# Another order of query tiles for attention's last two heads

## The chip, the cores and the metric

The kernel runs on one core of a Trainium2 chip. The metric is the device time of one execution in microseconds. Three runs of the kernel before took 2134.39 to 2135.3 us, with a median of 2135.06 us; beside them stands one execution under the profiler.

## The reference, cut to what matters

The program is one inference step of a two-layer decoder trunk over a prompt of 2048 positions and 64 sample positions, with 1024 channels. Layer 0 runs a pooling mixer and a differential attention side by side, layer 1 is a gated linear attention. The change touches the attention of the prompt and the output projection behind it:

```python
def block(args):                                   # 16 blocks of 128 queries
    qi, bi = args
    sc = jnp.einsum('bqhcd,bkhcd->bhcqk', qi, k)    # 4 heads, two score maps (c) each
    sc = jnp.where(causal, sc, -jnp.inf)
    p = jax.nn.softmax(sc, axis=-1)
    a = p[:, :, 0] - lam_full * p[:, :, 1]
    return jnp.einsum('bhqk,bkhe->bqhe', a, v)
...
o = rms_norm(o, subln_w) * (1.0 - lam_init)
mix = jnp.concatenate([pool_out * silu(pg), o * silu(ag)], axis=-1)
y = layer_norm(DN_ALPHA * x + mix @ w_out, ln_g, ln_b)
```

A block of queries needs no other block. Under the causal mask block t looks at t + 1 blocks of keys, so its work grows with t. A row of the output projection needs all four heads of its own position, and layer 1 needs the rows of layer 0.

## The kernel before, in words

Layer 0's input projection comes first, then attention head by head, each with other work woven in: head 0 with the pooling half of the output projection, head 1 with the sample positions, heads 2 and 3 together with the attention half of the output projection. That last stage, some 300 us long, is the one that changes. The first matmuls of layer 1 follow it.

A **tile** t is 128 queries, t from 0 to 15; two tiles with one number halved are a **pair** (pair 7 is tiles 14 and 15). Queries and gates are loaded by pairs, results are scaled by pairs. For one tile and one head `scores` makes two **score maps** (c = 0 and 1). From tile 8 on a map is four pieces of equal width, two to a PSUM tile of 128 x 2 x 512; there are two such PSUM tiles (`sc`, the pool has two buffers). For each piece TensorE multiplies the high and the low part of the queries with the keys (L1016, L1017), VectorE takes the maximum of a PSUM tile (L1021) and, with two of them, the smaller of the two negated maxima (L1034); ScalarE writes exp to SBUF (L1036), which frees the PSUM tile. VectorE then combines the two maps (L1045). Tiles 4 to 7 need one PSUM tile for a map, tiles 0 to 3 one for both.

`pv` follows a tile behind: transposes of 128 x 128 (L1068, `tp`), copies by ScalarE (L1073, `aT`), products with the values (L1061, `po`), and at the end of a pair the scale and the gate on GpSimd (`oq`, L1097 and L1099).

`out_attention` makes the **output tiles**. Number i is the 128 positions of tile i; number 16 is the sample. An output tile is four transposes (L1227, `otp`: two of the heads 0 and 1 that were stored, one each of heads 2 and 3), a split in high and low (L1231, L1232), 24 products of 512 columns (`op`, L51 to L53), sums on VectorE (L1281), a LayerNorm with three passes over 128 x 1024 on GpSimd (L1302 to L1304), a store, and eight transposes (L1245, `oyp`) for layer 1. It waits for `oq` of its pair and for its own loads (`om`, `oz`, three buffers for `oz`).

Two things set the order. `units` and `out_attention` are generators that `weave` draws from in proportion to their costs; an output tile is given out only when head 3 has finished the tile behind its pair (`A.done`). The instructions so recorded are then ordered by a scheduler with its own model of time; scores have a higher priority. Each engine works through its own list in that order. Before, tiles go 0 to 15 and output tiles 0 to 13, then 16, 14, 15.

Of the kernel before, what the change touches and what calls it, by code (L numbers as in the profile page):

```python
# [394 lines left out]
def layers(tc, d):  # L395
# [6 lines left out]
    with ExitStack() as left:  # L402
# [12 lines left out]
        for m, j in project_even(tc, d, P, P2, W, slot, psf):  # L415
# [8 lines left out]
            elif (m, j) == (5, 3):  # L424
                A.room_weights()
                units = A.units([0], [1])
# [15 lines left out]
    with ExitStack() as left:  # L442
        wp = left.enter_context(tc.tile_pool(name="aow", bufs=4, **rw))
        op = left.enter_context(tc.tile_pool(name="ao", bufs=2, **rw))
        sm = left.enter_context(tc.tile_pool(name="aosm", bufs=4, **rw))
        A.mixp = op
        O = Odd(tc, d, odd, keep, A.ident, P2, psf, fill_banks)

        def last():
            yield from A.units([2, 3], [])  # L450
            O.first_weights()
            yield from A.drain()
            A.over = True

        fill = out_attention(tc, d, A, wp, op, sm)
        weave(last(), fill, 2 * HEAD_COST, 17 * (8 * 640 + 1320.0), drain=False)
        right.close()
        O.start()
        for _ in fill:
            pass  # L460
# [423 lines left out]
class Attention:  # L884
# [166 lines left out]
    def pv(self, t, h, a, s1, place):  # L1051
# [51 lines left out]
            rs = slice(128 * (t - 1), 128 * t + 128)  # L1103
            nc.gpsimd.dma_start(self.d["mixa"][rs, 128 * h:128 * h + 128].rearrange("(c p) e -> p c e", p=128), oq)
        if h == 3:
            self.done = t
        yield 100

    def units(self, heads, after):


        for t in range(16):
            for h in heads:
                if t % 4 == 2 and t < 14:
                    self.load_kv(h, t // 4 + 1)
                if t % 2 == 1 and t < 15:
                    self.load_q(h, t // 2 + 1)
                if t == 14 and h == heads[0]:
                    for n in after:
                        self.load_kv(n, 0)  # L1120
                        self.load_q(n, 0)
                old = self.pend.pop(0) if len(self.pend) == 2 else None
                for c in self.scores(t, h):
                    yield c
                    c = next(old, None) if old else None
                    if c is not None:
                        yield c
                if old:
                    yield from old
                self.pend.append(self.pv(t, h, *self.cur))  # L1130
# [4 lines left out]
        self.pend = []  # L1135


HEAD_COST = 76000.0


# [55 lines left out]
def out_attention(tc, d, A, wp, op, sm):  # L1196
# [24 lines left out]
    def tile_(i, mt, m, z):  # L1221
        t0, n = TT[i]
        c = m.shape[1]
        tp = A.fill_tile(f"otp{i}")
        for k in range(4):
            src = m[:, 128 * k:128 * k + 128] if 128 * k < c else A.mix[i // 2, k][:, i % 2, :]
            nc.tensor.transpose(tp[:, 128 * k:128 * k + n], src, ident[:n, :n])  # L1227
        tv = tp.rearrange("p (k t) -> p k t", k=4)[:, :, :n]
        mh = op.tile([128, 4, 128], F32R, tag="oh", name=f"oh{i}")
        ml = op.tile([128, 4, 128], F32R, tag="ol", name=f"ol{i}") if i < 16 else mh[:, :, n:]  # L1230
        nc.scalar.activation(mh[:, :, :n], tv, AF.Copy)  # L1231
        nc.vector.tensor_tensor(out=ml[:, :, :n], in0=tv, in1=mh[:, :, :n], op=ALU.subtract)  # L1232
        yield 440
        ln = LayerNorm(tc, mt.bitcast(BF16)[:n], sm, z, 1.0, g[:n], b[:n], f"o0_{i}")
        yield from out_mm(nc, A.fill_tile, f"op{i}", n, mh, ml, w, ln.add)
        ln.finish(d["y0"][t0:t0 + n, :], i in (14, 15))
        zs[i] = z

    def turn(i):
# [9 lines left out]
            nc.scalar.dma_start(d["y0T"][4 * q:4 * q + 4, :, t0:t0 + n].rearrange("k p t -> p k t"), yt[:, :, :n])  # L1249
            yield 440  # L1250

    order = list(range(14)) + [16, 14, 15]
    ahead = load(order[0])
    for j, i in enumerate(order):
        while A.done < min((i | 1) + 1, 15) if i < 16 else not A.over:
            yield None
        now, ahead = ahead, load(order[j + 1]) if j < 16 else None
        yield from tile_(i, *now)
# [1176 lines left out]
```

## Time and profile before

| what | value |
|---|---|
| median of three runs | 2135.06 us |
| profiled execution, its own time | 2130.93 us |
| its span | 2129.1 us |
| mean granted TensorE clock | 0.981 |
| first and last score matmul of heads 2 and 3, tile 4 on | 907.66 and 1192 us |
| first product of output tile 14 | 1220.74 us |

The profile is read by engine: PE is TensorE's matmuls, PEld its weight loads, DVE is VectorE, ACT ScalarE, POOL GpSimd, SP the queue that issues most loads. A row of a timeline begins with the start and the duration in us; in square brackets stands how long the engine had been idle and what ended it. A row of a group ends with busy us, mean ns and idle us.

### The profile page before, as it was taken

The page shows a single profiled execution, that of the slowest core. Times are in us where ns is not written, and L with a number is a line of the kernel's source. Part 1 is how long each engine was busy: PE and PEld are TensorE (multiplying, and loading weights), DVE is VectorE, ACT ScalarE, POOL GpSimd, SP SyncE. Part 2 cuts the span into 40 slices and gives each one's busy share as a digit, 9 for nine tenths or more (in the row PEclk, how much of TensorE's full clock was granted, in tenths as well). Part 3 has the DMA queues.
Part 4 walks back from the last instruction along what each step waited for, and adds up shares of the span by engine and source line. Part 5 has one row for each costly group of instructions (what it writes and reads, how often), then busy time and mean ns, then how long its engine had stood idle before and what let it go on. Part 6 is the DMA issues. An engine that isn't in the chain of part 4 may idle for free.

```text
span 2129.1 us, 31464 instructions
## 1 busy us (share of the span) xinstructions
PE 1999.4 (94%) x10769; PEld 1633.9 (77%) x10769; DVE 1487.7 (70%) x2762; ACT 1022.1 (48%) x1922; POOL 876.6 (41%) x1163
## 2 busy tenths in 40 slices
PE   8999998999899999888898899999999898999998
PEld 7878786877688777667786688788887676788886
DVE  7697657564876676798767666666734547888884
ACT  4144433345633465664555533435527755555552
POOL 2345445323854542666543513222111122466554
PEclk9999999999999999999999999999999998999998
DMA  8877777447964598563321558665543457555532
GB/s 288 270 250 239 256 261 236 162 110 191 296 203 149 170 299 290 153 197 118 115 70 65 167 183 284 241 221 197 190 154 109 161 167 246 176 173 199 167 127 110
DMA packets 210972, 407.75 MB, mean 192 GB/s; under 512 B 29186, under 2 KB 106370, under 8 KB 210802
## 3 DMA queue, kind: packets, MB, share of 16 engines
q1 hardware_dynamic: 140354, 234.57, 36.2%
q0 software_dynamic: 49664, 156.39, 20.7%
q10 hardware_dynamic: 20784, 14.68, 2.2%
q8 instruction: 87, 1.43, 0.3%
q14 instruction: 83, 0.68, 0.1%
HBM read 277.99 MB, written 127.55 MB: 190 GB/s over the span
## 4 chain that ended last, share of the span: by engine, by line
PE 54%; DVE 15%; DMA 12%; issue 6%; ACT 6%; POOL 4%; SPq 1%; ACTq 0%; POOLq 0%; DVEq 0%
PE f L52 9%; PE f L51 9%; PE f L53 9%; PE po L1061 3%; PE sc L1016 2%; PE sc L1017 2%; ACT e L1036 2%; PE tp L1068 2%; DVE nm L1021 2%; DMA wr<-pt 2%; PE zp L51 1%; PE zp L53 1%; PE zp L52 1%; PE gz L53 1%; PE gz L51 1%
## 5 line engine op out<-in xcount | busy, mean ns | idle before, releaser
L1036 ACT ACTIVATE e<-sc,nm 128x896 f32<-128x896 f32 (+11 forms) x192 | 165.0, 865 | 126.4 <-DVE nm L1034 88.0
L1021 DVE TENSOR_REDUCE nm<-sc 128x1 f32<-128x768 f32 (+7 forms) x160 | 156.6, 990 | 27.1 <-PE sc L1017 16.7
L45 DVE TENSOR_TENSOR wk<-wr,wk 128x1024 fp32r<-128x1024 f32 x80 | 98.1, 1228 | 99.0 <-ACT wk L40 98.8
L45 DVE TENSOR_TENSOR wl<-wr,wh 128x1024 fp32r<-128x1024 f32 (+1 forms) x90 | 108.6, 1210 | 79.3 <-ACT wh L40 70.1
L1016 PE MATMUL sc<-kst,qh 128*128 128x512 f32 (+9 forms) x352 | 133.4, 382 | 29.7 <-ACT e L1036 28.3
L1061 PE MATMUL po<-vt,aT 128*128 128x128 f32 x1088 | 153.1, 280 | 3.6 <-ACT aT L1073 2.2
L40 ACT ACTIVATE wh<-wr 128x1024 fp32r<-128x1024 f32 (+1 forms) x85 | 88.0, 1038 | 137.3 <-PE f L52 67.6
L1061 PEld LDWEIGHTS po<-vt,aT 128*128 128x128 f32 x1088 | 138.1, 194 | 10.5 <-ACT aT L1073 2.5
L40 ACT ACTIVATE wk<-wr 128x1024 fp32r<-128x1024 f32 x77 | 81.2, 1058 | 131.1 <-PE f L53 94.0
L1073 ACT ACTIVATE aT<-tp 128x512 f32<-128x512 f32 (+3 forms) x160 | 85.5, 534 | 97.9 <-PE tp L1068 97.3
L1017 PE MATMUL sc<-kst,ql 128*128 128x512 f32 (+9 forms) x352 | 121.8, 349 | 0.0
L1016 PEld LDWEIGHTS sc<-kst,qh 128*128 128x128 f32 x352 | 67.5, 192 | 50.0 <-ACT e L1036 40.8
L1068 PE MATMUL tp<-ident,e 128*128 128x128 f32 x544 | 91.3, 282 | 12.1 <-ACT aT L1073 10.5
L1045 DVE SCALAR_TENSOR_TENSOR e<-e,c,e 128x128 f32<-128x128 f32 (+15 forms) x64 | 95.6, 1494 | 1.4
L1068 PEld LDWEIGHTS tp<-ident,e 128*128 128x128 f32 x544 | 63.8, 144 | 27.4 <-ACT aT L1073 15.4
L1017 PEld LDWEIGHTS sc<-kst,ql 128*128 128x128 f32 x352 | 67.7, 192 | 4.0 <-issue 0.2
L1039 DVE TENSOR_TENSOR s<-s 128x1 f32<-128x1 f32 x64 | 21.1, 330 | 68.3 <-ACT e L1036 68.0
L1092 POOL TENSOR_SCALAR s1q<-s 128x1 f32<-128x1 f32 x64 | 16.9, 267 | 102.6 <-DVE s L1039 87.6
L53 PE MATMUL op<-wh,ol 128*128 128x512 f32 x128 | 52.1, 407 | 5.0 <-DVE ol L1232 5.0
L51 PE MATMUL op<-wh,oh 128*128 128x512 f32 x128 | 53.0, 414 | 1.2 <-ACT oh L1231 1.1
L51 PE MATMUL zp<-wh,zh 128*128 128x512 f32 x128 | 52.1, 410 | 0.0
L51 PE MATMUL gz<-wh,gmh 128*128 128x512 f32 x128 | 51.6, 407 | 0.0
(882 smaller groups left out, 6669.7 us busy)
## 6 DMA issues: line engine op xcount, KB each, us to landing
wr<-in_w_q SPq DMA_DIRECT2D x75, 512.0 KB, 4.9
wr<-pt SPq DMA_DIRECT2D x40, 512.0 KB, 7.6
wr<-rt SPq DMA_DIRECT2D x40, 512.0 KB, 4.5
sk<-in_cachek SPq DMA_DIRECT2D x64, 256.0 KB, 3.8
sv<-in_cachev SPq DMA_DIRECT2D x64, 256.0 KB, 4.8
pt<-pn POOLq DMA_DIRECT2D x32, 256.0 KB, 7.0
qr<-q SPq DMA_DIRECT2D x64, 128.0 KB, 4.1
kr<-k SPq DMA_DIRECT2D x32, 256.0 KB, 4.5
```

The source lines that it names most:

```text
L40: h = nc.scalar.activation(hi, raw, AF.Copy)
L45: return h, (lo_eng or nc.vector).tensor_tensor(out=lo, in0=raw, in1=hi, op=ALU.subtract)
L51: nc.tensor.matmul(ps, lh(k), rh(k), start=(first and k == 0), stop=False, **kw)
L52: nc.tensor.matmul(ps, lh(k), rl(k), start=False, stop=False, **kw)
L53: nc.tensor.matmul(ps, ll(k), rh(k), start=False, stop=(last and k == n - 1), **kw)
L1016: nc.tensor.matmul(o, qh[:, c, qs], kst[:, ks], start=True, stop=False)
L1017: nc.tensor.matmul(o, ql[:, c, qs], kst[:, ks], start=False, stop=k < npc - 1)
L1021: nc.vector.tensor_reduce(out=nm[:, c, i:i + 1], in_=p[:, :, :w], op=ALU.max, axis=AX.XY, negate=True)
L1036: nc.scalar.activation(o, p, AF.Exp, bias=nm[:, m, 0:1], accum_out=s[:, m, i if npc > 1 else 0:][:, :1])
L1045: nc.vector.scalar_tensor_tensor(out=es[0][:, :nk], in0=es[1][:, :nk], scalar=c2, in1=es[0][:, :nk], op0=ALU.mult, op1=ALU.add)
L1061: nc.tensor.matmul(po, s[:, 128 * j:128 * j + 128], vt[:, k0 + j, :], start=(k0 + j == 0), stop=(k0 + j == n - 1))
L1068: nc.tensor.transpose(p[:, 128 * j:128 * j + 128], a[:, 128 * (k0 + j):128 * (k0 + j) + 128], self.ident)
```

## The change

`units` takes a list of tiles. Heads 2 and 3 get the list `TILES`, the pairs 0, 1, 2, 7, 3, 6, 4, 5 with two tiles each. `out_attention` goes through its output tiles by the same list, 16 ahead of the last two, and `A.done` counts finished tiles instead of naming the last one. Since tile 14 now comes seventh, the blocks of keys and values are asked for at positions 0, 1 and 3 of the list, where they were asked for at tiles 2, 6 and 10. The urgent form of the LayerNorm, which stays off GpSimd, goes with the last two of the list: 10 and 11.

```diff
-            yield from A.units([2, 3], [])
+            yield from A.units([2, 3], [], TILES)
...
         if h == 3:
-            self.done = t
+            self.done += 1
...
-    def units(self, heads, after):
-        for t in range(16):
+    def units(self, heads, after, order=range(16)):
+        order = list(order)
+        mixed = order != sorted(order)
+        for n, t in enumerate(order):
             for h in heads:
-                if t % 4 == 2 and t < 14:
-                    self.load_kv(h, t // 4 + 1)
-                if t % 2 == 1 and t < 15:
-                    self.load_q(h, t // 2 + 1)
+                if mixed:
+                    if n in (0, 1, 3):
+                        self.load_kv(h, 1 + (0, 1, 3).index(n))
+                elif n % 4 == 2 and n < 14:
+                    self.load_kv(h, n // 4 + 1)
+                if n % 2 == 1 and n < 15:
+                    self.load_q(h, order[n + 1] // 2)
...
+TILES = [t for i in (0, 1, 2, 7, 3, 6, 4, 5) for t in (2 * i, 2 * i + 1)]
...
-        ln.finish(d["y0"][t0:t0 + n, :], i in (14, 15))
+        ln.finish(d["y0"][t0:t0 + n, :], i in TILES[14:])
...
-    order = list(range(14)) + [16, 14, 15]
+    order = TILES[:14] + [16] + TILES[14:]
...
-        while A.done < min((i | 1) + 1, 15) if i < 16 else not A.over:
+        while A.done < min(TILES.index(i | 1) + 1, 15) if i < 16 else not A.over:
```

What this makes of the engines' lists is shown at three places. In the names the first number is the tile and the second the head; for scores the third is the map.

TensorE, around tile 14. Before, the second map of head 3 (`sc14_3_1`), up to tile 15:

```order
L1061 MATMUL po13_3_12191<-vt3_8755,aT13_3_12_12256 128x128 x2
L1227 MATMUL otp12_12469<-ident_4353,oq12_2_11841 128x128
L1016 MATMUL sc14_3_1_0_12221<-kst3_1_8747,qh3_7_11851 128x480
...
L1068 MATMUL tp14_2_0_12292<-ident_4353,e14_2_0_12083 128x128
L1016 MATMUL sc14_3_1_1_12238<-kst3_1_8747,qh3_7_11851 128x480
...
L1068 MATMUL tp14_2_0_12292<-ident_4353,e14_2_0_12083 128x128 x3
L1068 MATMUL tp14_2_4_12310<-ident_4353,e14_2_0_12083 128x128 x4
L1061 MATMUL po14_2_12291<-vt2_8735,aT14_2_0_12297 128x128 x4
L1016 MATMUL sc15_2_0_0_12285<-kst2_0_8726,qh2_7_11754 128x512
```

Now, the first map of head 2 (`sc14_2_0`) and what stands up to its second:

```order
L1016 MATMUL sc14_2_0_0_10189<-kst2_0_8726,qh2_7_9974 128x480
...
L1234 MATMUL otp1_9801<-ident_4353,om1_9745 128x128 x2
L1234 MATMUL otp1_9801<-ident_4353,oq0_2_9500 128x128
L1016 MATMUL sc14_2_0_1_10209<-kst2_0_8726,qh2_7_9974 128x480
...
L1061 MATMUL po4_3_10049<-vt3_8755,aT4_3_0_10055 128x128 x4
L51 MATMUL op1_0_9811<-wh101_9279,oh1_9806 128x512
...
L53 MATMUL op1_1_9825<-wh104_9305,ol1_9807 128x512
L1068 MATMUL tp5_2_0_10199<-ident_4353,e5_2_0_9982 128x128 x3
L1016 MATMUL sc14_2_1_0_10251<-kst2_1_8727,qh2_7_9974 128x480
```

Before, tile 14's four maps have no product of an output tile among them. Now all 24 products of output tile 1 stand between two maps of tile 14, and those of output tile 2 between the next two.

TensorE, behind the second map of tile 8 and head 3 (`sc8_3_1`). Before:

```order
L1017 MATMUL sc8_3_1_1_10732<-kst3_1_8747,ql3_4_10390 128x288
L1245 MATMUL oyp2_1_10269<-ident_4353,oz2_9767 128x128 x4
L1227 MATMUL otp4_10451<-ident_4353,om4_10121 128x128 x2
L1061 MATMUL po7_2_10546<-vt2_8735,aT7_2_4_10577 128x128 x4
L1068 MATMUL tp7_3_0_10650<-ident_4353,e7_3_0_10397 128x128 x4
L51 MATMUL op4_0_10461<-wh101_9271,oh4_10456 128x512
```

Now:

```order
L1017 MATMUL sc8_3_1_1_11796<-kst3_1_8747,ql3_4_11410 128x288
L1068 MATMUL tp13_3_4_11768<-ident_4353,e13_3_0_11417 128x128 x4
L1061 MATMUL po13_3_11749<-vt3_8755,aT13_3_0_11755 128x128 x4
L1068 MATMUL tp13_3_8_11785<-ident_4353,e13_3_0_11417 128x128 x4
L1061 MATMUL po13_3_11749<-vt3_8755,aT13_3_4_11773 128x128 x4
L1016 MATMUL sc9_2_0_0_11852<-kst2_0_8726,qh2_4_11312 128x320
```

Here 21 products of output tile 4 stood behind this map; now only transposes and value products of tile 13 do.

SP's list of loads, ahead of the first weight of the output projection (`wr101`). `kr2_3` is the last block of keys of head 2, `vt3` are values of head 3. Before:

```order
L963 DMA kr2_2_10153<-k0_58 64x2x512 x2
L963 DMA kr3_2_10249<-k0_58 64x2x512 x2
L989 DMA sga2_1_9450<-sg0_60 128x2x128
L963 DMA kr2_3_11015<-k0_58 64x2x512 x2
L963 DMA kr3_3_11152<-k0_58 64x2x512 x2
L951 DMA vt3_8755<-v0_59 128x4x128
L2246 DMA mixa_62<-ssq_9231 8x8x128 x4
```

Now:

```order
L989 DMA sga2_1_9474<-sg0_60 128x2x128
L977 DMA qr3_2_9701<-q0_57 64x2x256 x2
L963 DMA kr2_2_9459<-k0_58 64x2x512 x2
L963 DMA kr3_2_9507<-k0_58 64x2x512 x2
L963 DMA kr2_3_9641<-k0_58 64x2x512 x2
L963 DMA kr3_3_9693<-k0_58 64x2x512 x2
L951 DMA vt3_8755<-v0_59 128x4x128 x4
```

The scheduler had put the key loads this early already. Of the four value loads of head 3, two stood behind the output weights; now all four are ahead of them.

More of the change, by code (lines that the diff above doesn't have):

```diff
@@ L1105, in pv @@
         if h == 3:
-            self.done = t
+            self.done += 1
         yield 100
-    def units(self, heads, after):
-        for t in range(16):
+    def units(self, heads, after, order=range(16)):
+        order = list(order)
+        mixed = order != sorted(order)
+        for n, t in enumerate(order):
             for h in heads:
-                if t % 4 == 2 and t < 14:
-                    self.load_kv(h, t // 4 + 1)
-                if t % 2 == 1 and t < 15:
-                    self.load_q(h, t // 2 + 1)
[L1118 to L1121, printed above, removed]
+                if mixed:
[5 more added lines that the diff above has]
+                    self.load_q(h, order[n + 1] // 2)
+                if n == 14 and h == heads[0]:
+                    for x in after:
+                        self.load_kv(x, 0)
+                        self.load_q(x, 0)
                 old = self.pend.pop(0) if len(self.pend) == 2 else None
```

## The prediction

> **What bounds the kernel now.** I read the engine totals first, then the stage of heads 2 and 3 in stretches, then the starts of its score maps.
>
> ```profile
> PE 1999.4 (94%) x10769; PEld 1633.9 (77%) x10769; DVE 1487.7 (70%) x2762; ACT 1022.1 (48%) x1922; POOL 876.6 (41%) x1163
> ```
>
> TensorE is the busiest engine, but its busy time holds pipelined ends; what counts is how far apart matmuls start. The prices, from PE's timeline in the stage:
>
> ```profile
> 1128.09 0.39 PE L51 MATMUL op<-wh,oh 128*128 128x512 f32 x1
> 1128.32 0.39 PE L52 MATMUL op<-wl,oh 128*128 128x512 f32 x1
> ...
> 1133.26 0.60 PE L1068 MATMUL tp<-ident,e 128*128 128x128 f32 x4
> 1133.70 1.06 PE L1061 MATMUL po<-vt,aT 128*128 128x128 f32 x8
> 1134.59 0.60 PE L1245 MATMUL oyp<-ident,oz 128*128 128x128 f32 x4
> ```
>
> An output product costs 0.23 us (1128.32 - 1128.09); so do 512 columns of scores, and fewer in proportion. Four transposes cost 0.44. The eight value records cost 0.89; the program has four such products there, so one product is two records, 0.22. I call the sum of these prices of a stretch its work and the rest of its time its slack. The stretches of the stage (columns: us, then busy and count of PE, PEld, DVE, ACT, POOL, then granted clock, DMA share, GB/s):
>
> ```profile
> 907.66:934.20 26.54, 22.50 (x132) 18.60 (x133) 26.22 (x73) 17.40 (x41) 17.38 (x26) 0.94 0.85 269
> 934.20:955.81 21.61, 21.10 (x128) 16.81 (x126) 19.09 (x35) 14.37 (x30) 12.78 (x12) 1.00 0.29 91
> 955.81:1041.77 85.96, 77.81 (x492) 66.83 (x491) 68.96 (x146) 42.34 (x98) 55.27 (x53) 1.00 0.40 125
> 1041.77:1065.03 23.26, 18.46 (x117) 15.96 (x118) 18.82 (x41) 14.98 (x33) 13.10 (x16) 0.93 0.25 86
> 1065.03:1084.53 19.50, 19.50 (x121) 17.20 (x119) 10.97 (x27) 10.24 (x22) 8.06 (x7) 1.00 0.22 61
> 1084.53:1100.95 16.42, 14.58 (x101) 12.36 (x100) 13.09 (x28) 9.78 (x21) 10.06 (x11) 1.00 0.34 114
> 1100.95:1136.49 35.54, 32.86 (x205) 27.76 (x206) 23.71 (x48) 17.16 (x35) 13.02 (x13) 1.00 0.20 67
> 1136.49:1162.22 25.73, 18.05 (x104) 13.75 (x103) 19.58 (x34) 13.85 (x29) 11.40 (x15) 0.93 0.20 67
> 1162.22:1190.35 28.13, 27.56 (x169) 23.25 (x168) 22.92 (x37) 14.77 (x28) 8.60 (x7) 1.00 0.30 89
> 1190.35:1220.74 30.39, 20.03 (x144) 17.33 (x142) 17.81 (x39) 14.62 (x29) 19.41 (x19) 0.96 0.62 193
> ```
>
> I cut them where the order of the instructions changes character: a score map is **bare** when at most two products of an output tile stand behind its scores, and three stretches are runs of bare maps. Counting the records of each stretch at the prices above:
>
> | stretch | score maps | work | slack |
> |---|---|---|---|
> | 907.66, tiles 4 and 5 | 8 | 18.6 | 8.0 |
> | 934.20, tiles 6 and 7 | 8 | 19.9 | 1.7 |
> | 955.81, covered | 11 | 72.6 | 13.4 |
> | 1041.77, bare (tiles 10, 11) | 4 | 15.1 | 8.2 |
> | 1065.03, covered | 2 | 19.4 | 0.1 |
> | 1084.53, bare (tile 12) | 3 | 12.9 | 3.5 |
> | 1100.95, covered | 4 | 31.1 | 4.4 |
> | 1136.49, bare (tile 14) | 4 | 14.3 | 11.5 |
> | 1162.22, covered | 3 | 26.5 | 1.6 |
> | 1190.35, last map and tail | 1 | 18.2 | 12.2 |
>
> So the stage to 1190.35 has 230.4 us of PE work and 52.3 of slack. Bare runs hold 23.2 of it in 11 maps; the other 20 maps of the large tiles (8 to 15) hold 19.5, or 0.97 each. VectorE is no cover: in the bare runs it is busy less than the time too. What binds there is the chain of the softmax: both score tiles of a map stay occupied until exp has read them.
>
> ```profile
> 1012.82 0.39 PE L1016 MATMUL sc<-kst,qh 128*128 128x320 f32 x1
> ...
> 1017.69 0.43 PE L1016 MATMUL sc<-kst,qh 128*128 128x352 f32 x1
> ...
> 1026.97 0.43 PE L1016 MATMUL sc<-kst,qh 128*128 128x352 f32 x1 [0.48 <-ACT e L1036]
> ...
> 1031.92 0.38 PE L1016 MATMUL sc<-kst,qh 128*128 128x352 f32 x1
> ...
> 1046.81 0.44 PE L1016 MATMUL sc<-kst,qh 128*128 128x384 f32 x1 [0.38 <-ACT e L1036]
> ...
> 1053.60 0.44 PE L1016 MATMUL sc<-kst,qh 128*128 128x384 f32 x1 [2.92 <-ACT e L1036]
> ...
> 1151.08 0.49 PE L1016 MATMUL sc<-kst,qh 128*128 128x480 f32 x1 [2.00 <-ACT e L1036]
> ```
>
> The wait at a bare map's first matmul ends with ACT's exp (L1036). The links of the chain, by shape, over the stage:
>
> ```profile
> L1021 DVE TENSOR_REDUCE nm<-sc 128x1 f32<-128x1024 f32 x12 | 14.6, 1217 | 0.9 <-PE sc L1019 0.8
> L1021 DVE TENSOR_REDUCE nm<-sc 128x1 f32<-128x640 f32 x12 | 9.6, 816 | 0.0
> L1034 DVE TENSOR_TENSOR nm<-nm 128x1 f32<-128x1 f32 x32 | 8.9, 277 | 0.2
> L1036 ACT ACTIVATE e<-sc,nm 128x1024 f32<-128x1024 f32 x12 | 13.4, 1120 | 14.8 <-DVE nm L1034 11.7 <-DVE nm L1021 3.1
> L1036 ACT ACTIVATE e<-sc,nm 128x640 f32<-128x640 f32 x12 | 9.5, 804 | 3.4 <-DVE nm L1034 3.1 <-DVE nm L1021 0.2
> L1036 ACT ACTIVATION_READ_ACCUMULATOR e<-sc,nm 128x1 f32 x82 | 16.5, 201 | 0.0
> ```
>
> One map with pieces of width w: four score matmuls, one maximum of 2w, the minimum, two exps of 2w with their accumulator reads. At w = 512 that is 0.92 + 1.22 + 0.28 + 2 x (1.12 + 0.20) = 5.06 us, at 320 it is 0.58 + 0.82 + 0.28 + 2.01 = 3.69; by straight lines between: 3.45 at 288, 3.91 at 352, 4.14 at 384, 4.37 at 416, 4.60 at 448, 4.83 at 480. Measured periods lie above. The ten bare maps of 384 and up (1046.81 to 1065.03 and the two later runs) took 18.22 + 16.42 + 25.73 = 60.37 us against 3 x 4.14 + 3 x 4.37 + 4 x 4.83 = 44.85: 1.55 more per map, other work of DVE and ACT being queued between. The three narrow maps shown took 4.87, 4.95 and 5.04 against 3.69, 3.91, 3.91: 1.12 more.
>
> **The change part by part.** No arithmetic is added; the same tiles and output tiles come in another sequence.
>
> *Bare runs.* By the new order a run of five stands in tiles 8 and 9, one of three in tile 10, one of two in tile 13; tile 14's maps now alternate with output tiles 1 and 2. By the same prices the works are 5.01, 3.08, 3.74, 4.51, 3.07; 4.59, 2.08, 4.30; 4.60, 4.42. Periods, each no less than its work: 5.01 + 2 x 4.57 + 2 x 4.80 (the narrow excess 1.12), 3 x 5.03, 2 x 6.15 (the wide excess): 51.1 us against 39.4 of work, slack 11.7. That is 23.2 - 11.7 = **11.4 us less**. I take the narrow excess for seven of them since their width is that of the narrow maps shown; with 1.55 throughout it is 8.4 less. Nothing but exp hides this slack, and the output products that leave the small tiles are what fills tile 14.
>
> *Covered maps.* 21 instead of 20 large ones: 21 x 0.97 = 20.4, **0.9 more**. Bounds: the quietest stretch shown (1.6 in three maps, 0.53 each) gives 8.4 less, the first covered one (13.4 in 11, 1.22 each) 6.1 more.
>
> *Tiles 6 and 7.* Now they follow tile 15 and hold its value products, but only one output tile. Their maps had 1.7 / 8 = 0.21 each, those of tiles 4 and 5 had 8.0 / 8 = 1.00, under a VectorE that was busy for 26.22 of 26.54 us. Tiles 6 and 7 keep the same reductions and lose one output tile's VectorE work, so neither row fits; I take the middle, 0.6: 4.8 against 1.7, **3.1 more** (from 0 to 6.3).
>
> *Work and tail.* The last tile has 12 key blocks instead of 16, so eight transposes and eight value products move ahead of the last map: 8 x 0.11 + 8 x 0.22 = **2.65 more** there. Behind it the last head's chain shortens: eight score matmuls from 512 to 384 columns (0.46), maximum 0.27, two exps 0.42, the combination below, and one group of four transposes and four products (1.33).
>
> ```profile
> L1045 DVE SCALAR_TENSOR_TENSOR e<-e,c,e 128x1536 f32<-128x1536 f32 x2 | 3.6, 1812 | 0.0
> L1045 DVE SCALAR_TENSOR_TENSOR e<-e,c,e 128x2048 f32<-128x2048 f32 x1 | 2.3, 2340 | 0.0
> ```
>
> That is 2.34 - 1.81 = 0.53, in all **3.0 less** of the tail's 30.39. Cover of the tail (products of output tile 16, transposes of the row before) is unchanged: before tile 13, now tile 9.
>
> *Loads.* Keys are asked for at positions 0, 1 and 3 instead of tiles 2, 6 and 10, but SP's rows of key loads stand where they stood, ahead of the first output weights. Only two value loads of 256 KB are moved past those weights:
>
> ```profile
> 910.00:920.00 10.00, 7.67 (x51) 6.19 (x50) 10.00 (x27) 6.05 (x16) 4.85 (x5) 0.94 1.06 356
> ```
>
> At 356 GB/s they take 1.5 us. I count 0, since VectorE is full in that stretch whatever arrives, and 1.5 if the weights are late.
>
> *Sum:* -11.4 + 0.9 + 3.1 + 2.65 - 3.0 = **-7.8 us**. The profiled execution took 2130.93 us (span 2129.1), so 2123.2; the three timed runs have a median of 2135.06, 4.1 above it, and 2135.06 - 7.8 = 2127.3.
>
> The clock fell in two of the bare runs:
>
> ```profile
> 1050.00:1060.00 10.00, 7.08 (x43) 6.29 (x42) 7.86 (x18) 5.92 (x13) 6.78 (x10) 0.83 0.18 67
> 1150.00:1160.00 10.00, 6.62 (x27) 4.58 (x27) 6.87 (x14) 4.82 (x10) 1.98 (x4) 0.85 0.13 52
> ```
>
> The loss, 1.7 + 1.5 = 3.2 us of full clock, is inside the slack above, and in the sum it goes with the runs. The Trainium skill (TensorE: Matmul & The Clock Gate, "What's actually happening") puts the clock at half only after an idle window of about 3.4 us. By that, waits of 2.92 and 2.00 us would not be the cause. The rows don't settle it, since a wait recorded there starts at a modelled end; by the rule the sum would be 3.2 smaller.
>
> **The rivals.**
> 1. *The slack moves with the maps (no change).* There are 11 + 20 = 31 large maps before and 10 + 21 = 31 after. If slack belongs to the softmax chain of a map and not to bare runs, the 42.7 us stay, and 2.65 - 3.0 plus 0 to 3.1 give 2135 to 2138, say 2136. For it: single bare maps too had about 1.1 of excess. Against: 2.9 us per map in tile 14's run, 0.53 in tile 15's.
> 2. *POOL holds VectorE in the wide tiles (slower).* A LayerNorm's two passes on POOL stretch VectorE's one-column instructions:
>
> ```profile
> 1144.20 2.34 DVE L2317 TENSOR_TENSOR rmoa<-rmoa,rmra 128x2 f32<-128x2 f32 x1 [0.82 <-POOL rmoa L2325]
> ...
> 1148.78 1.07 DVE L1034 TENSOR_TENSOR nm<-nm 128x1 f32<-128x1 f32 x1
> ```
> ```profile
> 1144.13 2.39 POOL L1303 TENSOR_TENSOR oz<-oz,lng 128x1024 f32<-128x1024 f32 x1
> ...
> 1147.48 2.35 POOL L1304 TENSOR_TENSOR oz<-oz,lnb 128x1024 f32<-128x1024 f32 x1
> ```
>
>    Both ended with POOL's pass. Against the minimum's mean of 0.28 these are some 2.1 and 0.8, 2.9 us on the chain. Eight output tiles (1 to 5, 14, 15, 6) now pass during pairs 7 and 6, whose reductions are longest. If all eight pay 2.9 on the chain (23.2) in place of the 14 covered maps' 13.6 there, it is 9.6 more, and with the wide excess everywhere 12.6: -7.8 + 12.6 = +4.8, about 2140. It decides from seven of the eight on. Against: tile 15 took two output tiles with 1.6 of slack.
> 3. *Covered maps get quiet as well (more gain).* At 0.53 each: -7.8 - 9.3 = -17.1, so 2118. For it: output tiles now come one or two per tile, where tile 8 had nearly three.
> 4. *The clock dips stay* (the cause is not the bare runs; the page above): 3.2 of the gain is missing, -4.6, so 2130.5. A new run of five bare maps speaks for it, the narrow maps' shorter waits against.
>
> That the change would not do what it says (keys for tile 14 too late) is excluded by SP's order.
>
> **How the numbers follow.** Forecast 0.45 (own spread -3 to -11), rival 1 0.23, rival 2 0.15, rival 3 0.13, rival 4 0.04. The time is the forecast's, 2127. The range reaches over rival 3's time to 2116 and up to rival 1's and nearly rival 2's, 2139; both signs are in it, and the forecast's own range is 2124 to 2132. What a measurement can tell from no change is 0.2%, 4.3 us: faster is most of the forecast, rival 3 and half of rival 4, 0.54; same is the rest of these and nearly all of rival 1, 0.29; slower is rival 2 and a little of rival 1, 0.17.
>
> **What the new profile would show.** Tile 14's scores (480 columns) start early, with periods of 9 to 10 and 5 to 6 us in turn and no wait of 2 us for ACT; tiles 8 to 10 show bare maps with periods of 4.6 to 5.0. If those take 5.5 or more, the narrow excess was wrong. The tail from the last map's start to the products of output tile 10 is about 27.4 us. DVE one-column instructions of over 2 us in pair 7's tiles would speak for rival 2. The forecast is wrong if the slack of tiles 8 to 15, by the same prices, is not near 32 us, or if later stages change by more than a microsecond or two.

## The result, and the profile after

The changed kernel is slower. Its median is 2150.99 us (five executions, 2147.27 to 2152.76) against 2135.06 us for the kernel before on the same chip: a ratio of 1.0068, 95% interval 1.0051 to 1.0085. A second series gave 2148.47 us and 1.0063 (1.0048 to 1.0078). The forecast was 2127; 2151 lies above its range.

Both kernels were profiled twice (the second time among the experiments below), which shows how to read the difference. The first 320-column scores of the stage began at 907.66 and 917.37 us in the two profiles of the kernel before; from there on the two agree stretch by stretch within about a microsecond. So the scatter between executions lies ahead of this stage, and I cut the span from these scores on: up to the start of the last score map (A); the tail, up to the first product of the last but one output tile (B); up to the first product of layer 1's gated attention (C); and from there to the end (D). The stretches of the kernel before, first profile (columns as in the prediction):

```profile
907.66:1190.35 282.69, 252.42 (x1557) 212.53 (x1558) 223.37 (x465) 154.89 (x331) 149.67 (x156) 0.98 0.35 111
1190.35:1220.74 30.39, 20.03 (x144) 17.33 (x142) 17.81 (x39) 14.62 (x29) 19.41 (x19) 0.96 0.62 193
1220.74:1778.71 557.97, 542.65 (x2377) 442.30 (x2378) 333.86 (x496) 270.79 (x390) 114.10 (x199) 0.98 0.56 187
1778.71:2129.10 350.39, 326.17 (x1853) 271.19 (x1851) 273.88 (x553) 173.70 (x401) 187.65 (x140) 0.96 0.53 174
```

The same four of the changed kernel, whose profiled execution took 2147.27 us (span 2145.5):

```profile
908.39:1197.31 288.92, 255.95 (x1578) 217.22 (x1578) 216.52 (x472) 159.80 (x335) 149.03 (x157) 0.97 0.35 109
1197.31:1231.60 34.29, 18.82 (x123) 16.26 (x121) 19.71 (x34) 11.97 (x24) 21.36 (x21) 0.85 0.52 170
1231.60:1787.78 556.18, 541.65 (x2378) 440.92 (x2379) 333.88 (x496) 270.38 (x390) 114.39 (x199) 0.98 0.57 188
1787.78:2145.50 357.72, 327.37 (x1853) 272.79 (x1851) 275.19 (x553) 173.76 (x401) 190.83 (x140) 0.95 0.52 171
```

| stretch | before, twice | changed, twice | difference of the means |
|---|---|---|---|
| A, to the last map | 282.7, 282.7 | 288.9, 291.6 | +7.6 |
| B, tail | 30.4, 30.4 | 34.3, 34.3 | +3.9 |
| C | 558.0, 557.5 | 556.2, 557.2 | -1.0 |
| D, gated attention | 350.4, 351.6 | 357.7, 357.8 | +6.7 |

These make +17.2 where the medians of the two series differ by 15.9 and 12.9. (The two profiles of the changed kernel differ by 2.7 in A, more than any other pair in the table.) So the loss is in three places, and one of them, D, is a layer away from the edit.

**A.** Priced as in the prediction (work by prices, the rest is slack; now by the count of every record, which puts single values some tenths off the prediction's), the work to the last map went from 230.7 to 233.4 us. Slack by tile, in the order of the tiles before:

| tile | 4 | 5 | 6 | 7 | 8 | 9 | 10 | 11 | 12 | 13 | 14 | 15 | 8 to 15 |
|---|---|---|---|---|---|---|---|---|---|---|---|---|---|
| before | 6.0 | 2.2 | 0.6 | 1.0 | 3.6 | 6.6 | 4.6 | 6.3 | 3.6 | 4.5 | 11.5 | 1.4 | 42.1 |
| changed | 5.0 | 3.2 | 1.1 | 4.1 | 7.2 | 2.3 | 7.9 | 8.2 | 3.9 | 4.8 | 4.3 | 3.5 | 42.1 |

Tile 15's column ends where the last map starts in the row before, tile 11's in the row of the changed kernel. The second profiles gave 42.1 and 44.1 for tiles 8 to 15. Tile 14 became quiet, tiles 8, 10 and 11 became slack, and the sum did not fall. In the changed kernel, tile 14 (first), tile 8, and tile 10:

```profile
935.14:966.25 31.11, 27.98 (x167) 23.24 (x165) 24.17 (x49) 17.95 (x36) 19.70 (x19) 1.00 0.33 92
1089.77:1116.87 27.10, 21.75 (x152) 19.17 (x152) 19.00 (x36) 13.18 (x32) 12.91 (x11) 1.00 0.29 91
1140.25:1168.02 27.77, 23.74 (x146) 20.81 (x144) 20.96 (x42) 15.13 (x36) 18.85 (x20) 0.88 0.39 122
```

**B.** In the tail, VectorE's one- and two-column instructions on the chain of the last softmax and its row scale. Changed kernel:

```profile
1204.33 2.26 DVE L1039 TENSOR_TENSOR s<-s 128x1 f32<-128x1 f32 x1 [2.16 <-ACT e L1036]
1206.82 2.18 DVE L1044 SCALAR_TENSOR_TENSOR c<-s,nlam,c 128x1 f32<-128x1 f32 x1
1222.75 2.17 DVE L2319 TENSOR_TENSOR rmoa<-rmoa,ssq 128x2 f32<-128x2 f32 x1
1225.95 2.28 DVE L2324 TENSOR_TENSOR rmoa<-rmoa,rmra 128x2 f32<-128x2 f32 x1 [0.82 <-POOL rmoa L2332]
```

and what POOL did meanwhile (the LayerNorm of output tiles 9 and 16):

```profile
1204.21 2.36 POOL L1310 TENSOR_TENSOR oz<-oz,lng 128x1024 f32<-128x1024 f32 x1
1206.65 2.34 POOL L1311 TENSOR_TENSOR oz<-oz,lnb 128x1024 f32<-128x1024 f32 x1
1222.56 2.35 POOL L1310 TENSOR_TENSOR oz<-oz,lng 64x1024 f32<-64x1024 f32 x1
1225.87 2.34 POOL L1311 TENSOR_TENSOR oz<-oz,lnb 64x1024 f32<-64x1024 f32 x1
```

Each of the four starts inside a pass and ends with it. Undisturbed, such a row takes 0.2 us. The kernel before had two of them in its tail:

```profile
1196.29 2.29 DVE L1034 TENSOR_TENSOR nm<-nm 128x1 f32<-128x1 f32 x1
...
1214.15 2.23 DVE L2312 TENSOR_TENSOR rmoa<-rmoa,ssq 128x2 f32<-128x2 f32 x1
```

I call a one- to eight-column row of over 0.8 us *held*, and what it takes beyond 0.2 us its hold. The tail's holds are 4.1 us before and 8.1 after (8.0 in the second profile).

**D.** The tile scheduler wrote layer 1's gated attention in another order: of the 1852 TensorE rows there about 850 stand in another place, and no line of that code was touched. The place that shows it, before:

```profile
1799.89 0.66 PE L2011 MATMUL gmt<-ident,gm 128*128 128x128 f32 x4
...
1801.24 0.50 PE L51 MATMUL gz<-wh,gmh 128*128 128x512 f32 x1
```

and after:

```profile
1810.10 1.04 PE L2018 MATMUL gmt<-ident,gm 128*128 128x128 f32 x8
1813.74 0.50 PE L51 MATMUL gz<-wh,gmh 128*128 128x512 f32 x1 [2.61 <-ACT gmh L40]
...
1816.40 0.79 PE L53 MATMUL gz<-wh,gml 128*128 128x512 f32 x1 [1.47 <-DVE gml L45]
```

Before, six other products stand between the four transposes of `gm` and the first product (`gz`) that needs them split by ACT and VectorE. After, all eight transposes stand directly ahead of it, and TensorE waits 2.61 and 1.47 us. Behind these waits the granted clock falls. The seven microseconds from 27 us into D, before and after (the clock is the third figure from the end):

```profile
1805.71:1812.71 7.00, 6.36 (x36) 5.03 (x34) 6.84 (x16) 5.60 (x15) 3.94 (x4) 1.00 1.02 333
```
```profile
1814.78:1821.78 7.00, 5.53 (x14) 4.11 (x14) 5.26 (x9) 4.96 (x14) 4.41 (x3) 0.51 0.81 277
```

The second profiles show the same, 1.00 before and 0.56 after.

### The profile page after: what moved, and what is told of

It is laid out like the page before. It is cut to its first block, busy times and chain, and to the rows that moved or that the text cites. A ratio compares the mean times of both kernels' runs of the same rounds, so it can differ in the third digit from the quotient of the medians.

```text
span 2145.5 us, 31447 instructions
## 1 busy us (share of the span) xinstructions
PE 2005.0 (93%) x10769; PEld 1641.5 (77%) x10769; DVE 1483.4 (69%) x2762; ACT 1024.6 (48%) x1922; POOL 880.4 (41%) x1163
## 5 line engine op out<-in xcount | busy, mean ns | idle before, releaser
L1036 ACT ACTIVATE e<-sc,nm 128x896 f32<-128x896 f32 (+10 forms) x192 | 164.8, 863 | 120.7 <-DVE nm L1034 80.1
L45 DVE TENSOR_TENSOR wl<-wr,wh 128x1024 fp32r<-128x1024 f32 (+1 forms) x90 | 108.7, 1211 | 81.3 <-ACT wh L40 72.3
L1016 PE MATMUL sc<-kst,qh 128*128 128x384 f32 (+9 forms) x352 | 136.0, 389 | 30.1 <-ACT e L1036 29.3
L45 DVE TENSOR_TENSOR wk<-wr,wk 128x1024 fp32r<-128x1024 f32 x80 | 97.5, 1222 | 95.3 <-ACT wk L40 95.0
L1017 PE MATMUL sc<-kst,ql 128*128 128x384 f32 (+9 forms) x352 | 123.4, 353 | 0.0
L1092 POOL TENSOR_SCALAR s1q<-s 128x1 f32<-128x1 f32 x64 | 15.1, 236 | 99.1 <-DVE s L1039 83.3
L45 POOL TENSOR_TENSOR ql<-qr,qh 128x512 fp32r<-128x512 f32 x31 | 42.9, 1384 | 24.4 <-ACT qh L40 20.4
```

What stands on the lines that cost most here:

```text
L45: return h, (lo_eng or nc.vector).tensor_tensor(out=lo, in0=raw, in1=hi, op=ALU.subtract)
L1016: nc.tensor.matmul(o, qh[:, c, qs], kst[:, ks], start=True, stop=False)
L1017: nc.tensor.matmul(o, ql[:, c, qs], kst[:, ks], start=False, stop=k < npc - 1)
L1036: nc.scalar.activation(o, p, AF.Exp, bias=nm[:, m, 0:1], accum_out=s[:, m, i if npc > 1 else 0:][:, :1])
```

## The experiments

All of them. A, B, D as above, then the time from the first 320-column scores to the end and the slack of the large tiles, all from the one profile of each; then the median of the timed executions and its ratio to the kernel before of the same series.

| kernel | A | B | D | A to D | slack 8 to 15 | median us | ratio, interval |
|---|---|---|---|---|---|---|---|
| before | 282.7 | 30.4 | 350.4 | 1221.4 | 42.1 | 2135 | 1 |
| before, again | 282.7 | 30.4 | 351.6 | 1222.1 | 42.1 | 2141.31 (one execution) | |
| changed | 288.9 | 34.3 | 357.7 | 1237.1 | 42.1 | 2150.99 | 1.0068 (1.0051 to 1.0085) |
| changed, again | 291.6 | 34.3 | 357.8 | 1240.9 | 44.1 | 2148.47 | 1.0063 (1.0048 to 1.0078) |
| changed, LayerNorm of 8, 9, 16 on VectorE | 297.7 | 25.9 | 355.9 | 1239.1 | 46.1 | 2144.10 | 1.0042 (1.0023 to 1.0060) |
| changed, passes in quarters | 275.5 | 31.6 | 355.0 | 1218.6 | 27.1 | 2130.88 | 0.9974 (0.9959 to 0.9990) |
| changed, no passes | 271.9 | 22.5 | 350.2 | 1204.5 | 22.0 | 2117.13 | 0.9911 (0.9892 to 0.9930) |
| before, no passes | 259.3 | 27.2 | 353.8 | 1194.9 | 19.7 | 2110.14 | 0.9890 (0.9872 to 0.9907) |
| before, passes in quarters | 280.9 | 29.8 | 352.9 | 1218.2 | 39.8 | 2130.67 | 0.9989 (0.9973 to 1.0005) |
| pair 7 early, rest ascending, quarters | 268.7 | 33.8 | 358.4 | 1218.2 | 31.8 | 2128.46 | 0.9962 (0.9946 to 0.9979) |
| before, loads early | 286.1 | 32.4 | 357.5 | 1229.6 | 47.0 | 2140.80 | 1.0022 (1.0010 to 1.0034) |
| before, LayerNorm of 16 on VectorE | 282.6 | 29.4 | 361.1 | 1227.7 | 42.1 | 2138.47 | 1.0025 (1.0011 to 1.0039) |
| changed, LayerNorm of 16 on VectorE | 293.7 | 30.2 | 354.1 | 1232.0 | 45.6 | 2145.13 | 1.0059 (1.0040 to 1.0078) |
| pair 7 early, halves, 16 on VectorE | 282.1 | 31.5 | 356.9 | 1226.7 | 41.3 | 2132.97 | 0.9987 (0.9971 to 1.0003) |

**The LayerNorm of output tiles 8, 9 and 16 on VectorE**

```diff
-        ln.finish(d["y0"][t0:t0 + n, :], i in TILES[14:])
+        ln.finish(d["y0"][t0:t0 + n, :], i in TILES[12:] + [16])
```

> The changed kernel, with the LayerNorm of output tiles 8, 9 and 16 on VectorE (as that of the last two already is), so that no LayerNorm pass of POOL falls in the tail. Theory 'POOL holds VectorE in the tail': the four one-column VectorE rows of 2.2 us in the tail (1204, 1206, 1222 and 1225 us) go back to 0.2, about 8 us of holds less against 2 to 4 us of VectorE passes more on the chain: the tail falls from 34.3 to 28 to 31 us and the time by 3 to 6, to about 2146. Rival 'the tail is the softmax chain and the output tile, the holds are beside it': the tail stays within 1.5 us of 34.3 and the time within 2 of the changed kernel's 2151. The slack of tiles 8 to 15 (42.2 us) stays in both.

The tail's stretch in this kernel, and of TensorE's waits in it the longest:

```profile
1208.68:1234.56 25.88, 16.98 (x122) 14.81 (x121) 17.30 (x40) 11.73 (x24) 6.20 (x10) 0.98 0.60 181
```
```profile
PE otp L1234 <- POOL oq L1099: 4.6, 1, 4.6
```

The same wait in the changed kernel's tail:

```profile
PE otp L1234 <- POOL oq L1099: 8.4, 1, 8.4
```

No held row is left in the tail, and it took 25.9 us instead of 34.3, more than was expected. POOL was busy for 6.2 us there instead of 21.4, so the wait for the last gating (L1099) fell too. That the passes cost the tail its extra time is shown; holding VectorE and standing in POOL's own queue ahead of the gating are both in it. But stretch A grew by 8.8 over the first profile of the changed kernel (6.1 over the second): the slack of the large tiles rose to 46.1, by 4.0 and 2.0, and that of tiles 4 to 7 by 4.8 and 4.0. VectorE has six more instructions there in this version and POOL two fewer, and the granted clock in A is 0.954 where it was 0.970 and 0.965; which of these is a cause was not found.

**POOL's passes in quarters, after and before**

```diff
-        nc.gpsimd.tensor_tensor(out=z, in0=z, in1=self.g, op=ALU.mult)
-        nc.gpsimd.tensor_tensor(out=z, in0=z, in1=self.b, op=ALU.add)
+        parts = 4 if self.name.startswith("o0_") else 1
+        for x, op in ((self.g, ALU.mult), (self.b, ALU.add)):
+            for q in range(parts):
+                c = slice(1024 // parts * q, 1024 // parts * (q + 1))
+                nc.gpsimd.tensor_tensor(out=z[:, c], in0=z[:, c], in1=x[:, c], op=op)
```

> The changed kernel, with each of the two TENSOR_TENSOR passes that POOL makes for a LayerNorm of this stage (128x1024, 2.4 us) in four of 128x256 (0.6 us each by size, more by what one instruction costs). Theory 'POOL holds VectorE until its instruction ends': no one-column VectorE row in the stage is over 1.1 us; the tail falls by 3 to 6 us; if the holds also make the slack of the large maps, that falls from 42.2 by the 10 to 13 us that the stretched rows of tiles 8 to 15 hold, and the time is 2132 to 2140. Rival 'the slack is the softmax chain's own': tail as above, slack 39 or more, time 2144 to 2148. Rival 'the holds last as long as POOL is busy with such passes, whatever their size': the stretched rows stay.

> The kernel before, with POOL's two LayerNorm passes in quarters of 256 columns as in the second run. Theory 'POOL's long passes hold VectorE in both orders': leaving them out gained 34 us after the change and 25 before it, quarters gained 20 after it, so by the same share 15 here: 2120 (2116 to 2125), slack of tiles 8 to 15 from 42.3 to 27 to 32. Rival 'only the changed order suffers': 2132 or more, slack over 38. If this kernel is 6 us or more under the changed one with quarters (2131), the order itself costs that.

In the groups of the stage, changed kernel with quarters, then with whole passes:

```profile
L1314 POOL TENSOR_TENSOR oz<-oz,lnb 128x256 f32<-128x256 f32 (+1 forms) x60 | 51.2, 881 | 0.0
L1314 POOL TENSOR_TENSOR oz<-oz,lng 128x256 f32<-128x256 f32 (+1 forms) x60 | 45.7, 794 | 1.1
```
```profile
L1311 POOL TENSOR_TENSOR oz<-oz,lnb 128x1024 f32<-128x1024 f32 (+1 forms) x15 | 36.3, 2422 | 0.6
L1310 POOL TENSOR_TENSOR oz<-oz,lng 128x1024 f32<-128x1024 f32 (+1 forms) x15 | 35.7, 2379 | 1.2
```

The long holds went away as expected: to the last map five held rows with 4.5 us instead of eighteen with 22.0, none in the tail (before: four with 2.9 instead of 21 with 31.8). Shorter ones took their place. Counted from rows of 0.4 us on, the changed kernel has 39 with 19.6 us to the last map instead of 24 with 24.3, the kernel before 38 with 17.2 instead of 29 with 35.4, and every one of them ends with a POOL instruction. That VectorE is held until one POOL instruction ends, and not as long as POOL has passes to make, is shown. The changed kernel gained 18 to 20 us by the quarters (against its two medians), 15 to 17 of them as slack of its large tiles; its stage nearly kept its order (of 1700 TensorE rows in A and B some 150 stand in another place). The tail gained only 2.7: four quarters take 3.2 to 3.5 us in the mean where one pass took 2.4, and the gating still stands behind such work in POOL's queue:

```profile
PE otp L1234 <- POOL oq L1099: 8.8, 1, 8.8
```


The kernel before did not follow. It gained 5 us by the medians, with an interval that reaches to no change, where I had said 15; and its slack stayed at 39.8 although its holds had halved. The scheduler wrote its stage anew (some 630 of the 1700 rows stand in another place), and tile 12 in it has three bare maps in a row and 12.0 of slack, where 3.6 had been. So this run mixes shorter holds with another order, and the sum of the holds alone does not give the slack. With quarters, the two orders can't be told apart (0.9974 and 0.9989, overlapping).

**No passes, after and before**

```diff
-        nc.gpsimd.tensor_tensor(out=z, in0=z, in1=self.g, op=ALU.mult)
-        nc.gpsimd.tensor_tensor(out=z, in0=z, in1=self.b, op=ALU.add)
+        if not self.name.startswith("o0_"):
+            nc.gpsimd.tensor_tensor(out=z, in0=z, in1=self.g, op=ALU.mult)
+            nc.gpsimd.tensor_tensor(out=z, in0=z, in1=self.b, op=ALU.add)
```

> The changed kernel without those two POOL passes (the LayerNorm's gain and bias are left out for all output tiles but the last two). POOL then has 4.8 us less per output tile and never two inputs of 1024 columns. Theory 'the slack is the chain's own, POOL costs only in the tail': slack of tiles 8 to 15 39 or more, tail 25 to 28, time 2142 to 2146. Rival 'the passes make the slack of the covered maps': slack 28 to 33, time 2130 to 2136.

> The kernel before without those two POOL passes (gain and bias left out likewise). Theory 'the slack is the chain's own': slack of tiles 8 to 15 40 or more (42.7 in the kernel before), tail 26 to 28 instead of 30.4, time 2131 to 2133. Rival 'the passes make the slack': 20 us of stretched one-column rows in tiles 8 to 15 go, slack 25 to 32, time 2115 to 2125. If the changed order itself is what costs in the middle, the gap between this and the changed kernel without the passes stays 6 us or more; if the passes make the whole difference, it is under 3.

These kernels leave out the LayerNorm's gain and bias in this stage, for all output tiles but the last two; layer 1's LayerNorms keep theirs. The rival was right in both, and by more than it said: the passes make half of the slack. The groups of two of the one-column rows, first the kernel before, then without the passes:

```profile
L1044 DVE SCALAR_TENSOR_TENSOR c<-s,nlam,c 128x1 f32<-128x1 f32 x26 | 13.9, 533 | 0.5
L1039 DVE TENSOR_TENSOR s<-s 128x1 f32<-128x1 f32 x32 | 13.2, 411 | 31.7 <-ACT e L1036 31.5
```
```profile
L1044 DVE SCALAR_TENSOR_TENSOR c<-s,nlam,c 128x1 f32<-128x1 f32 x27 | 8.3, 308 | 0.3
...
L1039 DVE TENSOR_TENSOR s<-s 128x1 f32<-128x1 f32 x32 | 5.5, 171 | 35.8 <-ACT e L1036 35.8
```

In both lists of tiles the slack of tiles 8 to 15 falls to nearly the same value, 19.7 and 22.0, as it was the same with the passes. (The scheduler moved instructions in both: of the 1700 TensorE rows some 870 stand in another place in the first, some 240 in the second.) So the passes explain about half of that slack and not a difference between the orders in it. What remains between the two is 7 us by the medians and 7.9 in A and B together, and only 2.3 of it is in the large tiles. A and B without the passes, in the old order and in the changed one:

```profile
912.27:1171.59 259.32, 245.38 (x1548) 211.12 (x1548) 186.02 (x469) 156.10 (x332) 81.86 (x131) 0.99 0.39 124
1171.59:1198.78 27.19, 20.93 (x153) 18.36 (x151) 12.65 (x34) 13.64 (x27) 9.96 (x14) 1.00 0.56 174
```
```profile
911.01:1182.88 271.87, 256.19 (x1621) 219.14 (x1622) 191.41 (x481) 162.85 (x342) 89.63 (x136) 0.99 0.39 122
1182.88:1205.40 22.52, 12.36 (x78) 10.94 (x76) 9.32 (x24) 8.38 (x17) 8.15 (x11) 0.85 0.53 162
```

The chain of the last map is shorter in the changed order, as predicted (tail 22.5 against 27.2), but there are 10 us less of TensorE's work under it (8.9 against 19.3). Of these, 3.6 are the 16 products of output tile 16, which the scheduler had put ahead of the last map. So A is 12.6 us longer and the tail only 4.7 shorter: work that is taken from under the last chain has to be paid ahead of it.

**The late part: one line in each kernel, and second profiles**

```diff
-        ln.finish(d["y0"][t0:t0 + n, :], i in (14, 15))
+        ln.finish(d["y0"][t0:t0 + n, :], i in (14, 15, 16))
```

(for the changed kernel, `TILES[14:] + [16]`).

> The kernel before once more, for a second profile. From the start of layer 1's gated attention to the end the profiles so far took 357.7 and 357.8 us (changed kernel), 358.4 and 357.5 (the runs with pair 7 early and with the loads early, whose instructions stand there in the very order of the changed kernel), 350.4 and 350.2 (the kernel before, and the changed kernel without the passes, whose instructions stand there in the order of the kernel before). Theory 'the scheduler's order of that late part sets its time': 350 to 351.5 again, whatever the whole run takes. Rival 'scatter': anywhere from 350 to 358.

> The kernel before with the LayerNorm of output tile 16 on VectorE, as that of the last two is. One line; the attention stage keeps its order but for 22 instructions of TensorE, and the late part comes out in the very order of the changed kernel. Theory 'the late order costs': that part takes 357 to 358.5 us instead of 350.4, while the tail loses one hold of 2.2 us and POOL's queue ahead of the last gating (the 6.25 us wait falls to 3 to 4): 3 to 4 us less there; together 2137 to 2141. Rival 'the late order costs nothing': 2130 to 2133.

> The changed kernel once more, for a second profile. From the start of the gated attention of layer 1 to the end it took 357.7 us in the first profile against 350.4 in the kernel before. Theory 'this part of the loss comes with the kernel (the scheduler wrote that part in another order)': 355 to 360 again. Rival 'it is the scatter between executions': 348 to 353, the time then 3 to 6 lower. Time 2148 to 2153 by the first, and the slack of tiles 8 to 15 within 2 us of 42 in both.

> The changed kernel with the same one line. Its late part comes out close to the order of the kernel before (84 instructions of some 3200 stand otherwise). Theory: late part 350 to 354 us (357.7 before), tail 34.3 to 28 to 31 since two of its four holds of 2.2 us and the wait behind POOL's passes go; together 8 to 12 us less than the changed kernel: 2138 to 2143. Rival 'the late order costs nothing': only the tail's 4 to 6, 2144 to 2147. Slack of tiles 8 to 15 within 3 us of 42.

The kernel before with that line, at the place shown under D:

```profile
1797.58 1.04 PE L2011 MATMUL gmt<-ident,gm 128*128 128x128 f32 x8
1801.25 0.50 PE L51 MATMUL gz<-wh,gmh 128*128 128x512 f32 x1 [2.63 <-ACT gmh L40]
```

It has the changed kernel's order there, the changed kernel's wait, and 361.1 us in D, with the old tiles. Its stage up to the tail's end was 1.1 us shorter, where 3 to 4 had been expected, and it is slower as a whole by 1.0025. Sorted by the order of the late part, the fourteen profiles read:

| late part's order | D |
|---|---|
| as in the kernel before (three profiles) | 350.4, 351.6, 350.2 |
| the same but for 20 to 85 instructions (four) | 352.9, 353.8, 354.1, 356.9 |
| a third order (two) | 355.9, 355.0 |
| as in the changed kernel, to two instructions (five) | 357.7, 357.8, 358.4, 357.5, 361.1 |

Tiles, holds and loads of the stage are mixed in each row of this table: 350.2 belongs to the changed order of tiles (without passes), 357.5 and 361.1 to the old one. So stretch D follows the scheduler's order, and scatter doesn't reach from one end to the other. That is shown. All five profiles of the last row have the stretch of 6.8 us at half the granted clock, beginning 25.8 to 27.3 us into D; the three of the first row have none there. What in the stage's order tips the scheduler from one late order to another was not found.

In the changed kernel the line took 4.1 us from the tail (34.3 to 30.2; the wait for the last gating fell from 8.4 to 4.4) and 3.6 from D. The slack of the large tiles, though, came to 45.6 and A to 293.7, with TensorE's order in A and B the very same, and the time fell by 6 us at most, against the 8 to 12 expected. Why A is longer is open; the changed kernel's own profiles give 42.1 and 44.1.

**The loads alone**

```diff
-        mixed = order != sorted(order)
+        mixed = heads == [2, 3]
...
-TILES = [t for i in (0, 1, 2, 7, 3, 6, 4, 5) for t in (2 * i, 2 * i + 1)]
+TILES = [t for i in (0, 1, 2, 3, 4, 5, 6, 7) for t in (2 * i, 2 * i + 1)]
```

(Against the changed kernel: the tiles and output tiles come in the old order, and only the early loads stay.)

> The loads of the change alone: key and value loads of heads 2 and 3 asked for at the positions 0, 1 and 3 as in the changed kernel, with the tiles, output tiles and all else in ascending order. Theory (the prediction's term for the loads): no more than 1.5 us, 2133 to 2138. Rival 'the early loads stand in the way of output weights or queries': 2139 or more, and the first 320-column scores start 3 us or more later than at 907.7.

Slower by 1.0022 (1.0010 to 1.0034). The first 320-column scores started at 909.6, 2.0 us later than in the first profile before and 7.8 earlier than in the second, so nothing points to late weights. But the edit also gave the stage another order (tiles 12 and 14 hold 24.5 of 47.0 us of slack), and the late part the changed kernel's. It measures the scheduler, not the loads; the price of the loads alone is open.

**Half of the change, and a version of what helped**

```diff
-TILES = [t for i in (0, 1, 2, 7, 3, 6, 4, 5) for t in (2 * i, 2 * i + 1)]
+TILES = [t for i in (0, 1, 2, 7, 3, 4, 5, 6) for t in (2 * i, 2 * i + 1)]
```

with quarters; then the same with halves of 512 columns and output tile 16 on VectorE.

> Half of the change, with POOL's passes in quarters: pairs 0, 1, 2, 7, 3, 4, 5, 6, so the widest pair still comes early, the others ascend, and the last map has 14 key blocks. Theory 'the middle does not care about the order and the tail is the last map's chain less the work left under it': slack of tiles 8 to 15 within 4 us of the changed order's with quarters (29.4), last map's start to the last-but-one output tile 28 to 32, time between that of the kernel before with quarters and 2131. Rival 'the wide tiles early are what costs': as slow as 2131 or slower, with the loss in tiles 14 and 15.

> A version made of what helped: pairs 0, 1, 2, 7, 3, 4, 5, 6, POOL's passes in halves of 512 columns, the LayerNorm of output tile 16 on VectorE; its late part stands close to the order of the kernel before. Theory: late part 350 to 354, slack of tiles 8 to 15 between quarters and whole passes (33 to 40), 2118 to 2126, the fastest that keeps the arithmetic. Rival 'halves hold nearly as long as whole passes': slack 40 or more, 2127 to 2133.

The first has the lowest median of all versions that keep the arithmetic, 2128.46 us, 0.9962 (0.9946 to 0.9979) of the kernel before, with the slow late part still in it. That beats both kernels; from the two other kernels with quarters it can't be told apart (the intervals overlap). The widest tiles early do no harm: tiles 14 and 15 hold 1.3 and 1.4. Its tail, 33.8, was longer than forecast, with 25 us of TensorE busy in it. The second missed: with halves the slack is 41.3, as with whole passes, the late part took 356.9, and the time is that of the kernel before. The rival said so of the first and the last.

## Why the prediction was wrong

By its own steps:

*Bare runs, -11.4, and covered maps, +0.9: the step that failed.* I had put the slack of the large tiles down to runs of maps with little behind them, and expected near 32 us in all. It is 42.1 and 44.1, where 42.1 had been both times. The forecast for tile 14 itself held (11.5 to 4.3, no wait of 2 us for exp). By the prediction's own stretches the runs went from 23.4 us in 11 maps to 16.1 in the ten forecast (11.7 expected), 7.3 less; and the other large maps from 18.7 to 26.0, 7.3 more, which gave all of it back. The six single maps among them with at most two output products took 1.5 each, where four such had taken 0.6. Counted map by map, 15 of the 31 large maps to the last one had at most two output products in their period before, and 16 have after; their slack is 1.72 us each before and 1.55 after, and 1.02 and 1.15 in the others. Fourteen output tiles cover about half of the maps in both orders. By counting only runs as bare I let single ones pass as covered.

*The narrow excess of 1.12.* The run of five took 5.10, 4.45, 7.10, 5.70 and 3.59 us, 25.9 where I had 23.8; tile 10's three took 17.9 where I had 15.1. The 7.10 has a hold in it, a one-column sum that starts inside a pass and ends with it:

```profile
1110.47 1.87 DVE L1039 TENSOR_TENSOR s<-s 128x1 f32<-128x1 f32 x1 [1.68 <-ACT e L1036]
```
```profile
1109.96 2.36 POOL L1310 TENSOR_TENSOR oz<-oz,lng 128x1024 f32<-128x1024 f32 x1
```

So the excess that I read as "other work of DVE and ACT being queued between" was in good part POOL's passes: without them the maps with at most two output products have 0.89 of slack each in the changed order, where they had 1.55. In this run it depends on where a pass falls more than on the width of the map.

*Rival 1.* Rival 1 (the slack moves with the maps) was right for this stretch, to 2 us. It had 0.23.

*Tiles 6 and 7, +3.1.* Measured 1.6 to 5.2, +3.6, inside the bounds of 0 to 6.3. Mis-sized by 0.5.

*Work ahead of the last map, +2.65.* Measured +2.7.

*Tail, -3.0.* The second step that failed: +3.9. The tail does get shorter in the pair without passes (27.2 to 22.5, with less work under it). "Cover unchanged" was right for TensorE (18.2 before and 15.5 after, the difference being the last tile's own transposes and products, as forecast), but the sum left out what comes with that cover on POOL: the LayerNorm passes held VectorE four times instead of two, and TensorE's wait for the last gating, with passes ahead of it in POOL's queue, grew from 6.2 to 8.4. With the three LayerNorms on VectorE the tail took 25.9.

*Loads, 0.* Not settled, as told.

*"Later stages change by no more than a microsecond or two."* I named this as a sign of a wrong forecast and priced it at nothing. It is 6.7 us, two fifths of the loss. The order of the late part could be read ahead of any run.

*Rival 2, POOL holds VectorE.* The mechanism was right and the place wrong: in the wide tiles it did not decide (14 and 15 have 4.3 and 3.5 of slack, and no held row of over 2 us), in the tail it did. The Trainium skill (SBUF — State Buffer, "SBUF: two separate sides") has it as a rule: VectorE and GpSimd share one pair of ports, whoever starts first has it for its whole instruction, and a VectorE instruction with two inputs in SBUF, or in a mode that takes both ports, waits. The trace agrees (next section but one): 44 of the 45 held rows have two inputs in SBUF. The prediction had the holds of two rows in its text and put none into its sum.

So the sum: measured slack of large tiles 0.0 and +2.0 (two profiles) in place of -10.5, tiles 6 and 7 +3.6 in place of 3.1, tiles 4 and 5 0.0 and +0.8 in place of 0, work +2.7 in place of 2.65, tail +3.9 in place of -3.0, late part +6.7 and C -1.0 in place of 0. That is +16 to +19 for the -7.8 of the forecast.

The clock was not in the tail's loss: the changed kernel's tail took 34.29 us at a granted 0.85 and 34.26 at 0.75. In the late part it comes with the waits shown under D. In A the dips of rival 4 stayed and grew: by the granted clock 8.5 and 10.2 us of full speed were lost there, where it had been 5.1 and 6.7; what share of the slack that makes was not separated.

## What to carry to other kernels

Slack that belongs to the chain of each unit of work comes along when the units are put in another order; before pricing an order by its bad runs, count units by what stands behind each of them, with the single ones. Where a scheduler writes the program, look at the order of everything that follows the edit, since a stage that no line touches can be written worse, here by 7 us of 2135. And an elementwise pass on POOL is paid on VectorE's chain: what it may hold there belongs into the sum, and its length is worth trying as a size.

## What the runs showed of the hardware

- All 23 held rows of the kernel before, and all 22 of the changed one, start inside a POOL instruction and end within 0.03 us of its end: 35 of the 45 with a LayerNorm's TENSOR_TENSOR, 7 with the splitting of queries (L45), 3 with a one-input TENSOR_SCALAR. Of the short VectorE rows that start inside a LayerNorm pass with over 1 us of it to come, 32 of 33 with two inputs are held; all ten reciprocals among them, which have one input, take 0.15 to 0.17 us, and the one TENSOR_SCALAR was held. Longer rows with two inputs are held too: the sum of squares over 128x128 took up to 2.49 us where it takes 0.27 alone. VectorE's rows that read PSUM are not held: the maximum over 128x1024 took 1.22 us with the passes and without them.
- A pass over 64 partitions takes as long as one over 128 (2.35 and 2.36 us), and one over 256 columns 0.79 to 0.88 us in the mean (0.73 in the median), a third of one over 1024 and not a quarter. Short POOL instructions release VectorE sooner and cost POOL more.
- Two executions of one program can differ by 10 us ahead of a stage and agree within 0.02 us in it (282.69 and 282.71, 30.39 and 30.38). It is not always so close: the changed kernel's two gave 288.9 and 291.6 for A. Stretches between landmarks tell more than spans.
